# A hybrid attention block on one core: attention B normalised from split squares, and three stretches re-ordered

## The chip, the cores and the metric

The kernel runs on one core of one Trainium2 chip. The metric is device time in microseconds (us) of one execution; shorter is better. Before the change three runs took 741.76, 742.28 and 742.61 us, so the median is 742.28.

## What is computed

One layer for 512 tokens of width 1024, in float32: a combined projection of x, two attentions side by side, gates, an output projection, LayerNorm, a squared-ReLU MLP (1024 to 4096 to 1024) and a second LayerNorm. The part that the change rewrites is the end of attention B, which has four heads of value width 128:

```
def rms_norm(x, g):
    return x * lax.rsqrt(jnp.mean(jnp.square(x), axis=-1, keepdims=True) + RMS_EPS) * g

w   = softmax(q1 k1) - lam * softmax(q2 k2)          # per head, causal by chunks of 64
out = rms_norm(w @ v, subln_g) * (1 - lam_init)      # over the 128 columns of a head
```

Queries and keys of B are rotated first: of each 64 columns the first 16 are turned by an angle that depends on the position (`partial_rope`). Attention A has eight heads with a bias table and no rotation.

## The kernel before

Every float32 product is made of three matmuls. Each operand is split into a high part (a cast to fp32r on ACT, `split`, L82) and the rest (a subtraction on DVE, L83); then high times high, high times low and low times high are summed in PSUM. A matmul takes 128 rows by 512 columns. Weights come from memory as chunks of 128x1024 (`prefetch`, L107), each landing in one of three `raw` buffers and being split into one of three `wh` and three `wl` buffers; `chunk` (L144) hands out the next one and prefetches.

The order of the program: some matmuls on zeros while the first loads come in (`warm_up`); the projection, written as a generator (`proj`) that is advanced one step at a time; attention A in 36 steps with one projection step between two of them; attention B (`attn_b`) in 16 units (head, block of 128 queries) and a tail, with 1.8 projection steps between two units; then the two branch products, the output projection in two column groups, LayerNorm 1 inside the second group, the MLP and LayerNorm 2. Instructions are issued by a scheduler that keeps one order per engine: it may move an instruction ahead of others of its engine by its own priorities, unless `tc.keep_in_program_order` pins it. An engine then runs its list strictly in order, waiting where an operand or a buffer isn't ready.

A unit of B works as follows. PE makes two score blocks in `st` banks (L270, L271); DVE adds the mask and takes the maximum (L278), ACT takes exp (L280), DVE the reciprocal of the 128x1 sums (L282), POOL multiplies one map (L575), DVE subtracts (L576). Three units later (`LAG`) PE transposes the result (L289) into one of four `mm` banks, ACT copies it to `ph` (L296) and DVE writes the rest to `pl` (L297), which frees the bank. After the fourth unit of a head PE multiplies with the values (`pv`, L511 to L513) into `o`. `mean_sq` squares on ACT (L516), sums over the 128 rows of the head with eight plain matmuls of two columns against ones (L524), and computes 1/sqrt by an integer start and three Newton steps on 128x8 numbers (L527 to L538, thirteen DVE instructions). `normalise` spreads the 512 factors over all rows: POOL multiplies the identity with them (L547, two products), PE multiplies with ones (L552, two matmuls), and DVE forms the product with the head's output (L554), which is split.

The rotation (`rope`, L476) is four POOL instructions for a query or key tile, eight calls in all. The LayerNorm 1 part (`fin1`) adds on DVE (L735), takes statistics (L739), normalises (L805 on ACT, L806 on DVE), and PE transposes the rows (L817).

Of the kernel before, what the change touches and what calls it, by code (L numbers as in the profile page):

```python
# [40 lines left out]
def block_kernel(ctx, tc, w, x_t, x, pos, relb, bgate, lq1, lk1, lq2, lk2, subg,  # L41
# [38 lines left out]

    def split(src, h, l, eng=None):
        A.copy(out=h, in_=src)  # L82
        (eng or V).tensor_tensor(out=l, in0=src, in1=h.bitcast(F32), op=ALU.subtract)  # L83
# [4 lines left out]
    def load_x(k, cuts=((0, S),)):  # L88
        if k not in x_raw:
            x_raw[k] = e_tile()  # L90
        for lo, hi in cuts:
            nc.sync.dma_start(out=x_raw[k][:, lo:hi], in_=x_t[k * P:(k + 1) * P, lo:hi])
# [13 lines left out]

    def prefetch(n_dma, n_split):  # L107
        while dma_at[0] < min(NCH, n_dma):
            i = dma_at[0]
            raws[i] = wp.tile([P, 1024], F32, tag="raw", bufs=3, name=name("raw"))  # L110
            if i == 0:
                for j in range(2):
                    sl = slice(512 * j, 512 * (j + 1))
                    if j == 0:
                        load_x(0, ((0, P),))
                    nc.sync.dma_start(out=raws[i][:, sl], in_=w[i][:, sl])
                    load_x(j, ((P, S),) if j == 0 else ((0, S),))
            else:
                nc.sync.dma_start(out=raws[i], in_=w[i])
            dma_at[0] += 1  # L120
        while split_at[0] < min(NCH, n_split):
            i = split_at[0]
            if i in dest:
                hs, ls = dest[i]
                for j in range(2):
                    split(raws[i][:, 512 * j:512 * (j + 1)], hs[j], ls[j],
                          G if i in on_pool else V)
                parts[i] = (hs, ls)
            else:
# [26 lines left out]
    A.activation(ones_r, ones, AF.Copy, scale=128.0)  # L156
# [30 lines left out]
    def s_group(act_h, act_l, evac, before=None, nk=4, tail=1, cut_last=False):  # L187
# [13 lines left out]
        for c in range(nk):  # L201
            if before:
                before(c)
            wh, wl = chunk()
# [271 lines left out]
    def rope(t):  # L476
# [3 lines left out]
        G.tensor_tensor(out=a, in0=v[:, :, :, 0:16], in1=cos_t, op=ALU.mult)  # L480
# [16 lines left out]
    def attn_b():  # L497
# [3 lines left out]
        for which in range(2):  # L501
            rope(qb[which][0])
        ops[0] = prep_b(0)
        yield

        def pv(h):
# [8 lines left out]
            sq = e_tile()  # L515
            A.activation(sq, o, AF.Square)  # L516
            og = e_tile()
            A.activation(og, o, AF.Copy, scale=g8)
            return og, sq

        def mean_sq(og, sq):
            ms = mm_bank()
            for t in range(NT):
                T.matmul(ms[:, 2 * t:2 * t + 2], sq[:, t * P:(t + 1) * P], ones[:, 0:2],  # L524
                         start=True, stop=True)
            v, y, a = small(8), small(8), small(8)
            V.tensor_scalar(v, ms[:, 0:8], EPS, None, op0=ALU.add)  # L527
            V.tensor_scalar(y.bitcast(I32), v.bitcast(I32), -0.5, float(0x5f3759df),
                            op0=ALU.mult, op1=ALU.add)
            for _ in range(3):  # L530
                V.scalar_tensor_tensor(out=a, in0=y, scalar=-0.5, in1=y,
                                       op0=ALU.mult, op1=ALU.mult)
                V.tensor_tensor(out=a, in0=a, in1=v, op=ALU.mult)
                V.scalar_tensor_tensor(out=y, in0=a, scalar=1.5, in1=y,
                                       op0=ALU.add, op1=ALU.mult)
            rh, rl = small(8, FR), small(8, FR)
            V.tensor_copy(out=rh, in_=y)
            V.tensor_tensor(out=rl, in0=y, in1=rh.bitcast(F32), op=ALU.subtract)  # L538
            return og, sq, rh, rl

        def normalise(og, a, rh, rl):
            rb = mm_bank()
            for n, part in enumerate((rh, rl)):
                diag = vt()
                r = part.bitcast(F32)
                eye = ident[:, :]
                G.tensor_tensor(out=diag.rearrange("p (t q) -> p t q", q=P),  # L547
                                in0=bass.AP(tensor=eye.tensor, offset=eye.offset,
                                            ap=[eye.ap[0], [0, NT], [1, P]]),
                                in1=bass.AP(tensor=r.tensor, offset=r.offset,  # L550
                                            ap=[r.ap[0], [2, NT], [0, P]]), op=ALU.mult)
                T.matmul(rb, ones_r, diag, start=(n == 0), stop=(n == 1))  # L552

            V.tensor_tensor(out=a.rearrange("p (q n) -> p n q", n=NT),  # L554
                            in0=og.rearrange("p (n q) -> p n q", q=P),
                            in1=rb.rearrange("p (n q) -> p n q", q=P), op=ALU.mult)
            h_, l_ = vt(), vt()
            split(a, h_, l_)
            ob_h.append(h_)
            ob_l.append(l_)  # L560

        held = {}
        for i in range(len(units) + LAG + 7):
# [25 lines left out]
            for stage in (6, 3, 1):  # L589
                k = i - LAG - stage  # L590
                if 0 <= k < len(units) and k % NT == NT - 1:
# [3 lines left out]
                    elif stage == 3:  # L595
                        held[h] = mean_sq(*held[h])
# [65 lines left out]

    A.preload_act_table(AF.Exp)
    warm_up(6)
    prefetch(1, 0)
    rope_angles()
# [6 lines left out]
    advance(7)  # L673
# [7 lines left out]
    for i in range(36):  # L681
        next(steps_a, None)
        advance(1)
        if i == 32:
# [3 lines left out]
    for _ in range(16 + LAG + 7):  # L688
# [146 lines left out]
    for n, _ in enumerate(s_group(mh, ml, evac_res(0))):  # L835
        prefetch(c0 + 5, min(c0 + 3, next_chunk[0] + 3))
# [7 lines left out]
    for _ in s_group(mh, ml, fin1, tail=4):  # L844
# [141 lines left out]
```

## Time and profile before

| | |
|---|---|
| median of 3 runs | 742.28 us |
| profiled execution | 741.43 us |
| its span in the trace | 739.6 us |
| mean granted TensorE clock | 0.997 of full speed |

The span runs from the first to the last instruction of the trace; 1.8 us of the profiled execution lie around it. The trace gives each engine's instructions with start and length; PE is TensorE, DVE VectorE, ACT ScalarE, POOL GpSimd, SP the engine that issues most DMAs. Matmuls overlap, so what one costs is read from the distance between two starts, not from its length. An idle time in brackets is followed by what ended it.

### The profile page before, as it was taken

The numbers are of one execution on the slowest core, as the hardware profiler recorded it, in microseconds if no ns is written. First come the engines' busy times: TensorE is split into PE (matmuls) and PEld (weight loads), VectorE is DVE, ScalarE is ACT, GpSimd is POOL, SyncE is SP. The second block draws the span as 40 slices with busy tenths as digits, with TensorE's granted clock in tenths as the row PEclk, the third lists the DMA queues.
The fourth block names the chain that finished last, engine by engine and source line by source line (L and its number), as shares of the span: only waits on it lengthen the run. The fifth ranks groups of instructions, "written<-read, shape, count | busy, mean of one in ns | idle before, by whom it ended". The sixth has DMA issues, their size and how long they took to land.

```text
span 739.6 us, 9267 instructions
## 1 busy us (share of the span) xinstructions
PE 725.7 (98%) x3446; PEld 606.0 (82%) x3446; DVE 423.4 (57%) x831; ACT 283.6 (38%) x497; POOL 94.4 (13%) x127
## 2 busy tenths in 40 slices
PE   8999999999999999999999999999999999999995
PEld 6888888878888888888788888888888888888885
DVE  6566655546666764746876886423135655612545
ACT  5565654536565643224363223221212322312200
POOL 0023333550122121143000000000000000000001
PEclk9999999999999999999999999999999999999998
DMA  8553222212332222182502232322223223232302
GB/s 294 197 173 112 85 88 60 83 58 86 121 108 86 86 63 104 62 313 96 190 1 84 87 114 86 115 86 98 102 86 113 86 86 113 86 113 86 115 29 85
DMA packets 26940, 78.34 MB, mean 106 GB/s; under 512 B 4368, under 2 KB 5136, under 8 KB 26896
## 3 DMA queue, kind: packets, MB, share of 16 engines
q1 hardware_dynamic: 26176, 76.71, 31.3%
q10 hardware_dynamic: 720, 1.05, 0.4%
q8 instruction: 27, 0.44, 0.2%
q14 instruction: 17, 0.14, 0.1%
HBM read 71.45 MB, written 2.10 MB: 99 GB/s over the span
## 4 chain that ended last, share of the span: by engine, by line
PE 87%; DVE 4%; POOL 3%; ACT 2%; DMA 2%; issue 1%; SPq 0%; DVEq 0%; ACTq 0%; POOLq 0%
PE mm L178 11%; PE mm L180 11%; PE mm L179 11%; PE mm L183 7%; PE mm L185 7%; PE mm L184 7%; PE st L185 3%; PE st L184 3%; PE st L183 3%; PE st L180 3%; PE st L179 3%; PE st L178 3%; POOL G L629 2%; DMA raw<-in_w_dram 2%; PE st L271 1%; PE o L185 1%
## 5 line engine op out<-in xcount | busy, mean ns | idle before, releaser
L83 DVE TENSOR_TENSOR wl<-raw,wh 128x1024 fp32r<-128x1024 f32 (+1 forms) x115 | 140.2, 1219 | 128.5 <-ACT wh L82 128.4
L82 ACT CAST wh<-raw 128x1024 fp32r<-128x1024 f32 (+1 forms) x115 | 120.0, 1044 | 207.6 <-PE st L185 67.1
L183 PE MATMUL mm<-wh,X 128*128 128x512 f32 (+1 forms) x192 | 77.0, 401 | 1.9 <-ACT X L82 1.6
L178 PE MATMUL mm<-X,wh 128*128 128x512 f32 x192 | 76.9, 401 | 0.0
L179 PE MATMUL mm<-X,wh 128*128 128x512 f32 x192 | 74.9, 390 | 0.0
L180 PE MATMUL mm<-X,wl 128*128 128x512 f32 x192 | 74.9, 390 | 0.0
L184 PE MATMUL mm<-wl,X 128*128 128x512 f32 (+1 forms) x192 | 74.5, 388 | 0.0
L185 PE MATMUL mm<-wh,X 128*128 128x512 f32 (+1 forms) x192 | 74.2, 388 | 0.0
L783 POOL TENSOR_SCALAR s<-s 128x1 f32<-128x1 f32 x1 | 0.4, 409 | 388.8 <-DVE s L767 388.8
L178 PE MATMUL mm<-x1t_h,wh 128*128 128x512 f32 x128 | 49.8, 389 | 0.0
L179 PE MATMUL mm<-x1t_l,wh 128*128 128x512 f32 x128 | 49.8, 389 | 0.0
L180 PE MATMUL mm<-x1t_h,wl 128*128 128x512 f32 x128 | 49.8, 389 | 0.0
L280 ACT ACTIVATE e<-e,s 128x128 f32<-128x128 f32 (+3 forms) x64 | 36.1, 564 | 30.4 <-DVE s L278 30.0
L372 POOL TENSOR_SCALAR e<-e,s 128x128 f32<-128x128 f32 (+3 forms) x32 | 34.7, 1085 | 76.3 <-DVE s L282 76.3
L183 PEld LDWEIGHTS mm<-wh,X 128*128 128x128 f32 x192 | 36.2, 189 | 9.8 <-ACT X L82 2.7
L185 PEld LDWEIGHTS mm<-wh,X 128*128 128x128 f32 x192 | 36.0, 188 | 7.8 <-DVE X L83 0.3
L180 PEld LDWEIGHTS mm<-X,wl 128*128 128x128 f32 x192 | 36.0, 188 | 7.7
L178 PEld LDWEIGHTS mm<-X,wh 128*128 128x128 f32 x192 | 36.1, 188 | 6.9
L184 PEld LDWEIGHTS mm<-wl,X 128*128 128x128 f32 x192 | 36.2, 188 | 6.7 <-DVE wl L83 0.2
L179 PEld LDWEIGHTS mm<-X,wh 128*128 128x128 f32 x192 | 36.2, 188 | 6.5
L82 ACT CAST V<-lt 128x512 fp32r<-128x512 f32 x24 | 14.9, 621 | 62.8 <-DVE lt L858 62.8
L180 PE MATMUL st<-x1t_h,wl 128*128 128x512 f32 (+1 forms) x104 | 38.8, 373 | 0.0
(257 smaller groups left out, 1537.0 us busy)
## 6 DMA issues: line engine op xcount, KB each, us to landing
raw<-in_w_dram SPq DMA_DIRECT2D x119, 512.0 KB, 3.3
q<-q SPq DMA_DIRECT2D x32, 128.0 KB, 2.3
G<-in_relb_dram SPq DMA_DIRECT2D x8, 256.0 KB, 4.2
x<-in_x_dram SPq DMA_DIRECT2D x4, 512.0 KB, 7.6
e<-in_x_t_dram SPq DMA_DIRECT2D x7, 256.0 KB, 6.4
out_dram<-x SPq DMA_DIRECT2D x3, 256.0 KB, 2.0
out_dram<-x ACTq DMA_DIRECT2D x3, 256.0 KB, 2.1
raw<-in_w_dram SPq DMA_DIRECT2D x2, 256.0 KB, 3.2
```

The lines of the kernel that those rows point to most:

```text
L82: A.copy(out=h, in_=src)
L83: (eng or V).tensor_tensor(out=l, in0=src, in1=h.bitcast(F32), op=ALU.subtract)
L178: T.matmul(ps, lw_h, rh, start=first, stop=False)
L179: T.matmul(ps, lw_h, rl, start=False, stop=False)
L180: T.matmul(ps, lw_l, rh, start=False, stop=last)
L183: T.matmul(ps, ah, w_h, start=first, stop=False)
L184: T.matmul(ps, ah, w_l, start=False, stop=False)
L185: T.matmul(ps, al, w_h, start=False, stop=last)
L271: T.matmul(ps[:, :n], q2[:, sl], k1[:, :n], start=False, stop=True)
L280: A.activation(e[:, :n], e[:, :n], AF.Exp, bias=nm, scale=-1.0, accum_out=sums)
L372: G.tensor_scalar(ex[:, :n], ex[:, :n], r, None, op0=ALU.mult)
L629: G.tensor_tensor(out=m, in0=m, in1=g, op=ALU.add)
```

## The change

Four things change. (1) `pv` writes the squares twice on ACT, once as fp32 and once as fp32r, and DVE subtracts: a high and a low part. `normalise` sums them over the rows with two 128x512 matmuls against a matrix of 1/128, which at once spreads the mean over all rows; ACT takes the square root (with its table of functions loaded before, and the exp table again behind), DVE the reciprocal of all 128x512 numbers, and DVE multiplies. `mean_sq`, its matmuls, the Newton steps and the POOL products are gone, and normalising a head starts three units earlier. (2) Three weight splits of the first MLP chunks are pinned behind each step of LayerNorm 1. (3) The rotations are pinned: head 0's two at steps 22 and 30 of attention A, the others at the start of units 0 and 1 of the head before. (4) The first 128 columns of x^T are loaded by ACT's queue, chunk 1 of the weights is loaded and split in halves between the x^T pieces, rotary angles come later, and seven warm-up matmuls read a 128x128 tile.

```diff
@@ -78,18 +78,22 @@
     def o_bank():
         return bank("o")
 
+    pinned = [False]
+
     def split(src, h, l, eng=None):
         A.copy(out=h, in_=src)
-        (eng or V).tensor_tensor(out=l, in0=src, in1=h.bitcast(F32), op=ALU.subtract)
+        i = (eng or V).tensor_tensor(out=l, in0=src, in1=h.bitcast(F32), op=ALU.subtract)
+        if pinned[0]:
+            tc.keep_in_program_order(i)
+    def first_loads():
+
+        load_x(0, ((0, P),), A)
+        for i in range(2):
+            raws[i] = wp.tile([P, 1024], F32, tag="raw", bufs=3, name=name("raw"))
+            for j in range(2):
+                sl = slice(512 * j, 512 * (j + 1))
+                nc.sync.dma_start(out=raws[i][:, sl], in_=w[i][:, sl])
+                load_x(2 * i + j, ((P, S),) if i + j == 0 else ((0, S),))
+        dma_at[0] = 2
+
     def prefetch(n_dma, n_split):
         while dma_at[0] < min(NCH, n_dma):
             i = dma_at[0]
             raws[i] = wp.tile([P, 1024], F32, tag="raw", bufs=3, name=name("raw"))
-            if i == 0:
-                for j in range(2):
-                    sl = slice(512 * j, 512 * (j + 1))
-                    if j == 0:
-                        load_x(0, ((0, P),))
-                    nc.sync.dma_start(out=raws[i][:, sl], in_=w[i][:, sl])
-                    load_x(j, ((P, S),) if j == 0 else ((0, S),))
-            else:
-                nc.sync.dma_start(out=raws[i], in_=w[i])
+            nc.sync.dma_start(out=raws[i], in_=w[i])
...
-                if i == 0:
+                if i < 2:
                     for j in range(2):
                         sl = slice(512 * j, 512 * (j + 1))
                         split(raws[i][:, sl], h[:, sl], l[:, sl])
-                        split_x(j)
+                        split_x(2 * i + j)
                 else:
...
     def chunk(ahead=2):
         c = next_chunk[0]
-        prefetch(c + ahead + 1, c + ahead)
+        prefetch(c + ahead + 1, c + max(ahead, 1))
         next_chunk[0] += 1
         return parts.pop(c)
...
     def warm_up(n):
         ps = st_bank()
-        src = e_tile()
-        V.memset(src, 0.0)
+        src = e_tile()[:, 0:P].bitcast(FR)
+        V.memset(src.bitcast(F32), 0.0)
+        wide = bass.AP(tensor=src.tensor, offset=src.offset, ap=[src.ap[0], [0, NT], [1, P]])
         for _ in range(n):
-            T.matmul(ps, src[:, 0:P].bitcast(FR), src.bitcast(FR), start=True, stop=True)
+            T.matmul(ps.rearrange("p (a b) -> p a b", b=P), src, wide, start=True, stop=True)
...
-        G.tensor_tensor(out=a, in0=v[:, :, :, 0:16], in1=cos_t, op=ALU.mult)
+        tc.keep_in_program_order(
+            G.tensor_tensor(out=a, in0=v[:, :, :, 0:16], in1=cos_t, op=ALU.mult))
...
             rope(qb[which][0])
+            yield
         ops[0] = prep_b(0)
...
-            sq = e_tile()
+            sq, sq_h, sq_l = e_tile(), vt(), vt()
             A.activation(sq, o, AF.Square)
+            A.activation(sq_h, o, AF.Square)
             og = e_tile()
             A.activation(og, o, AF.Copy, scale=g8)
-            return og, sq
-
-        def mean_sq(og, sq):
-            ms = mm_bank()
-            for t in range(NT):
-                T.matmul(ms[:, 2 * t:2 * t + 2], sq[:, t * P:(t + 1) * P], ones[:, 0:2],
-                         start=True, stop=True)
-            v, y, a = small(8), small(8), small(8)
...
-            rh, rl = small(8, FR), small(8, FR)
-            V.tensor_copy(out=rh, in_=y)
-            V.tensor_tensor(out=rl, in0=y, in1=rh.bitcast(F32), op=ALU.subtract)
-            return og, sq, rh, rl
-
-        def normalise(og, a, rh, rl):
+            V.tensor_tensor(out=sq_l, in0=sq, in1=sq_h.bitcast(F32), op=ALU.subtract)
+            return og, sq, sq_h, sq_l
+
+        def normalise(og, a, sq_h, sq_l):
+
             rb = mm_bank()
...
-                                            ap=[eye.ap[0], [0, NT], [1, P]]),
-                                in1=bass.AP(tensor=r.tensor, offset=r.offset,
-                                            ap=[r.ap[0], [2, NT], [0, P]]), op=ALU.mult)
-                T.matmul(rb, ones_r, diag, start=(n == 0), stop=(n == 1))
-
-            V.tensor_tensor(out=a.rearrange("p (q n) -> p n q", n=NT),
+            for n, part in enumerate((sq_h, sq_l)):
+                T.matmul(rb, ones_r, part, start=(n == 0), stop=(n == 1))
+            A.activation(a, rb, AF.Sqrt, bias=epst)
+            V.reciprocal(a, a)
+
+            b = e_tile()
+            V.tensor_tensor(out=b.rearrange("p (q n) -> p n q", n=NT),
                             in0=og.rearrange("p (n q) -> p n q", q=P),
-                            in1=rb.rearrange("p (n q) -> p n q", q=P), op=ALU.mult)
+                            in1=a.rearrange("p (n q) -> p n q", q=P), op=ALU.mult)
             h_, l_ = vt(), vt()
-            split(a, h_, l_)
...
-        for i in range(len(units) + LAG + 7):
+        for i in range(len(units) + LAG + 4):
             if i < len(units):
                 h, t = units[i]
                 n = (t + 1) * P
+                if t < 2 and h < 3:
+                    rope(qb[t][h + 1])
...
-                if t == 1 and h < 3:
-                    for which in range(2):
-                        rope(qb[which][h + 1])
...
-            for stage in (6, 3, 1):
+            for stage in (3, 1):
                 k = i - LAG - stage
                 if 0 <= k < len(units) and k % NT == NT - 1:
                     h = units[k][0]
                     if stage == 1:
                         held[h] = pv(h)
-                    elif stage == 3:
-                        held[h] = mean_sq(*held[h])
                     else:
...
         def before(c):
-            if c:
+            for k in (2 * c + 2, 2 * c + 3):
+                if 0 < c and k < KD:
+                    load_x(k)
+            if c > 1:
                 for k in (2 * c, 2 * c + 1):
-                    load_x(k)
                     split_x(k)
         yield from s_group(xh, xl, evac_va, before)
...
-    A.preload_act_table(AF.Exp)
-    warm_up(6)
-    prefetch(1, 0)
-    rope_angles()
+    warm_up(7)
+    first_loads()
+    tc.keep_in_program_order(A.preload_act_table(AF.Exp))
     main = proj()
 
     def advance(n):
         for _ in range(n):
             next(main, None)
 
-    advance(7)
+    advance(2)
+    tc.keep_in_program_order(A.activation(ones_r, ones, AF.Copy, scale=1.0))
+    rope_angles()
+    advance(5)
     rope_tables()
     lam_and_gains()
     advance(1)
@@ -681,11 +669,11 @@
     for i in range(36):
         next(steps_a, None)
         advance(1)
-        if i == 32:
...
     for n, _ in enumerate(s_group(mh, ml, evac_res(0))):
-        prefetch(c0 + 5, min(c0 + 3, next_chunk[0] + 3))
+        prefetch(c0 + 5, min(c0 + 4, next_chunk[0] + 3))
     fin = evac_res(1)
 
     def fin1(s, ps, lo, hi):
@@ -841,7 +829,10 @@
         ln1(s)
         if s:
             x1_transposed(s - 1)
-    for _ in s_group(mh, ml, fin1, tail=4):
+        pinned[0] = True
+        prefetch(c0 + 7, c0 + 4 + min(s + 1, 3))
+        pinned[0] = False
+    for _ in s_group(mh, ml, fin1, tail=4, ahead=0):
```

The start, on SP, the loads behind the first x^T and weight pieces (`raw` weights, `e` x^T pieces); first before, then after:

```order
L119 DMA raw_168<-in_w_dram 128x1024
L119 DMA raw_170<-in_w_dram 128x1024
L92 DMA e_216<-in_x_t_dram 128x512
L92 DMA e_222<-in_x_t_dram 128x512
L119 DMA raw_228<-in_w_dram 128x1024
L92 DMA e_258<-in_x_t_dram 128x512
L92 DMA e_264<-in_x_t_dram 128x512
```
```order
L96 DMA e_116<-in_x_t_dram 128x512
L118 DMA raw_118<-in_w_dram 128x512
L96 DMA e_120<-in_x_t_dram 128x512
L118 DMA raw_118<-in_w_dram 128x512
L96 DMA e_123<-in_x_t_dram 128x512
L126 DMA raw_130<-in_w_dram 128x1024
L403 DMA s_187<-in_pos_dram 128x4
L96 DMA e_232<-in_x_t_dram 128x512
L96 DMA e_234<-in_x_t_dram 128x512
```

The third x^T piece stood behind both whole weight chunks (1024 columns each); it now stands behind half a chunk (512 columns).

The end of attention A, on POOL (L480 to L485 are one rotation, `e` tiles at L372, after at L379, are attention's multiplies); before, then after:

```order
L480 TENSOR_TENSOR s_2209<-G_1490,cos_t 128x128
L481 TENSOR_TENSOR s_2210<-G_1490,sin_t 128x8x8
L483 TENSOR_TENSOR s_2210<-G_1490,sin_t 128x8x8
L485 TENSOR_TENSOR G_1490<-s_2209,s_2210 128x8x16
L480 TENSOR_TENSOR s_2487<-G_1184,cos_t 128x128
L481 TENSOR_TENSOR s_2488<-G_1184,sin_t 128x8x8
L372 TENSOR_SCALAR e_1561<-e_1561,s_1566 128x128
L483 TENSOR_TENSOR s_2488<-G_1184,sin_t 128x8x8
L485 TENSOR_TENSOR G_1184<-s_2487,s_2488 128x8x16
```
```order
L379 TENSOR_SCALAR e_1519<-e_1519,s_1524 128x512
L379 TENSOR_SCALAR e_1571<-e_1571,s_1576 128x128
L379 TENSOR_SCALAR e_1609<-e_1609,s_1614 128x256
L379 TENSOR_SCALAR e_1638<-e_1638,s_1643 128x384
L488 TENSOR_TENSOR s_1671<-G_1498,cos_t 128x128
L489 TENSOR_TENSOR s_1672<-G_1498,sin_t 128x8x8
L491 TENSOR_TENSOR s_1672<-G_1498,sin_t 128x8x8
L493 TENSOR_TENSOR G_1498<-s_1671,s_1672 128x8x16
L379 TENSOR_SCALAR e_1680<-e_1680,s_1685 128x512
L488 TENSOR_TENSOR s_1855<-G_1186,cos_t 128x128
```

Three rotations and more stood directly ahead of the multiply of e_1561; now the same multiply (e_1571) has attention's multiplies ahead of it, and the rotation of G_1498 comes three multiplies later.

The normalising of head 0, on DVE (s 128x8 are the Newton steps; e_2368 the squares, then the root, then its reciprocal); before, then after:

```order
L297 TENSOR_TENSOR pl_2346<-mm_2499,ph_2345 128x3x128
L527 TENSOR_SCALAR s_2510<-mm_2505 128x8
L282 RECIPROCAL s_2481<-s_2478 128x1
L528 TENSOR_SCALAR s_2511<-s_2510 128x8
L574 TENSOR_SCALAR s_2483<-s_2481,lam 128x1
L531 SCALAR_TENSOR_TENSOR s_2512<-s_2511 128x8
L533 TENSOR_TENSOR s_2512<-s_2512,s_2510 128x8
L534 SCALAR_TENSOR_TENSOR s_2511<-s_2512,s_2511 128x8
L576 SCALAR_TENSOR_TENSOR e_2466<-e_2466,s_2471,e_2476 128x256
L531 SCALAR_TENSOR_TENSOR s_2512<-s_2511 128x8
L533 TENSOR_TENSOR s_2512<-s_2512,s_2510 128x8
L534 SCALAR_TENSOR_TENSOR s_2511<-s_2512,s_2511 128x8
```
```order
L304 TENSOR_TENSOR pl_2350<-mm_2507,ph_2349 128x3x128
L538 RECIPROCAL e_2368<-e_2368 128x512
L289 RECIPROCAL s_2501<-s_2498 128x1
L541 TENSOR_TENSOR e_2518<-e_2373,e_2368 128x4x128
L563 TENSOR_SCALAR s_2503<-s_2501,lam 128x1
L285 ISA e_2566,s_2567<-st_2563,maskb 128x384
L285 ISA s_2567 128x1
L565 SCALAR_TENSOR_TENSOR e_2486<-e_2486,s_2491,e_2496 128x256
L85 TENSOR_TENSOR V_2521<-e_2518,V_2520 128x512
L262 SCALAR_TENSOR_TENSOR q_2592<-mm_2587,q_2592 64x512
L289 RECIPROCAL s_2571<-s_2568 128x1
L285 ISA e_2576,s_2577<-st_2573,maskb 128x384
```

And on ACT in the same place, before, then after:

```order
L280 ACTIVATE e_2466,s_2468<-e_2466,s_2467 128x256
L296 CAST ph_2345<-mm_2499 128x3x128
L280 ACTIVATE e_2476,s_2478<-e_2476,s_2477 128x256
L607 ACTIVATE G_2565<-mm_2540,bg 128x512
L280 ACTIVATE e_2570,s_2572<-e_2570,s_2571 128x384
L254 ACTIVATE q_2596<-mm_2591 64x512
L296 CAST ph_2345<-mm_2619 128x4x128
L280 ACTIVATE e_2580,s_2582<-e_2580,s_2581 128x384
```
```order
L287 ACTIVATE e_2486,s_2488<-e_2486,s_2487 128x256
L303 CAST ph_2349<-mm_2507 128x3x128
L537 ACT_TABLE_LOAD
L537 ACTIVATE e_2368<-mm_2513,epst 128x512
L287 ACT_TABLE_LOAD
L287 ACTIVATE e_2496,s_2498<-e_2496,s_2497 128x256
L591 ACTIVATE G_2561<-mm_2536,bg 128x512
L261 ACTIVATE q_2592<-mm_2587 64x512
L84 CAST V_2520<-e_2518 128x512
L303 CAST ph_2349<-mm_2615 128x4x128
```

The short Newton rows are replaced by one 128x512 reciprocal and the product, ahead of the mask rows (L285) and of the last `pl`; on ACT two table loads and the root stand ahead of the unit's second exp.

## Rows read from the trace of the kernel before

**Rows 1.** The page: PE's busy line, and GB/s in forty slices.
```profile
PE 725.7 (98%) x3446; PEld 606.0 (82%) x3446; DVE 423.4 (57%) x831; ACT 283.6 (38%) x497; POOL 94.4 (13%) x127
...
GB/s 294 197 173 112 85 88 60 83 58 86 121 108 86 86 63 104 62 313 96 190 1 84 87 114 86 115 86 98 102 86 113 86 86 113 86 113 86 115 29 85
```
**Rows 2.** Timeline of ACT (start, length, instruction, idle and releaser), 10.0 to 12.2.
```profile
10.48 1.04 ACT L82 CAST wh<-raw 128x1024 fp32r<-128x1024 f32 x1 [0.60 <-DMA raw<-in_w_dram]
11.44 1.14 ACT L82 CAST X<-e 128x512 fp32r<-128x512 f32 x2
```
**Rows 3.** Timeline of PE, 9.8 to 12.6.
```profile
10.09 0.40 PE L185 MATMUL mm<-wh,X 128*128 128x512 f32 x1
12.10 0.50 PE L183 MATMUL mm<-wh,X 128*128 128x512 f32 x1 [1.61 <-ACT X L82]
```
**Rows 4.** Timeline of POOL, 140 to 152.5: first rotation row, attention A's multiply behind the rotations.
```profile
140.67 0.46 POOL L480 TENSOR_TENSOR s<-G,cos_t 128x128 f32<-128x128 f32 x1 [0.81 <-ACT G L467]
...
151.32 0.60 POOL L372 TENSOR_SCALAR e<-e,s 128x128 f32<-128x128 f32 x1
```
**Rows 5.** Timeline of PE, 148.5 to 153.5.
```profile
150.33 0.39 PE L271 MATMUL st<-q,q 128*128 128x512 f32 x1
151.98 0.33 PE L289 MATMUL st<-ident,e 128*128 128x128 f32 x1 [1.25 <-POOL e L372]
...
152.76 0.50 PE L352 MATMUL o<-pl,V 128*128 128x512 f32 x1 [0.22 <-DVE pl L297]
```
**Rows 6.** Timeline of PE, 226.5 to 228.
```profile
226.85 0.95 PE L524 MATMUL mm<-ones,e 128*128 128x2 f32 x8
227.67 0.48 PE L178 MATMUL mm<-X,wh 128*128 128x512 f32 x1
```
**Rows 7.** Groups of DVE by line and form: count, busy us, mean ns, idle before.
```profile
L533 DVE TENSOR_TENSOR s<-s,s 128x8 f32<-128x8 f32 x12 | 2.0, 167 | 0.4
...
L554 DVE TENSOR_TENSOR e<-e,mm 128x512 f32<-128x512 f32 x4 | 4.2, 1062 | 0.0
...
L83 DVE TENSOR_TENSOR V<-e,V 128x512 fp32r<-128x512 f32 x8 | 5.5, 686 | 1.4 <-ACT V L82 1.4
...
L282 DVE RECIPROCAL s<-s 128x1 f32<-128x1 f32 x64 | 10.3, 161 | 21.0 <-ACT e L280 16.1 <-POOL e L372 4.6
...
L447 DVE TENSOR_SCALAR lam<-lam 128x1 f32<-128x1 f32 x1 | 0.2, 153 | 0.0
L449 DVE TENSOR_SCALAR g<-g 128x1 f32<-128x1 f32 x1 | 0.1, 146 | 0.0
```
**Rows 8.** Timeline of ACT, at heads 0, 1 and 2, and at the last table load.
```profile
228.05 0.47 ACT L296 CAST ph<-mm 128x384 fp32r<-128x384 f32 x1
...
233.41 0.69 ACT L607 ACTIVATE G<-mm,bg 128x512 f32<-128x512 f32 x1 [3.98 <-PE mm L180]
...
254.43 0.46 ACT L296 CAST ph<-mm 128x384 fp32r<-128x384 f32 x1
...
279.33 0.47 ACT L296 CAST ph<-mm 128x384 fp32r<-128x384 f32 x1
...
313.43 1.28 ACT L697 ACT_TABLE_LOAD   x1
```
**Rows 9.** DVE's busy time in one stretch: window, length, busy us and instructions.
```profile
229.12:237.22 8.10, 5.48 (x25) 1.00 0.20 67
```
**Rows 10.** Timeline of PE, at heads 0, 1 and 2.
```profile
238.89 0.27 PE L289 MATMUL mm<-ident,e 128*128 128x128 f32 x1
...
267.99 0.40 PE L512 MATMUL o<-pl,V 128*128 128x512 f32 x1
...
291.38 0.39 PE L512 MATMUL o<-pl,V 128*128 128x512 f32 x1
```
**Rows 11.** Timeline of DVE, 362.5 to 364.
```profile
362.69 1.21 DVE L83 TENSOR_TENSOR wl<-raw,wh 128x1024 fp32r<-128x1024 f32 x1
```
**Rows 12.** Waits of PE: line, releaser, us in total, times, longest.
```profile
PE mm L817 <- ACT lt L805: 1.0, 1, 1.0
```

More of the change, by code (lines that the diff above doesn't have):

```diff
@@ L79, in o_bank, with load_x @@
         return bank("o")
+    pinned = [False]
     def split(src, h, l, eng=None):
         A.copy(out=h, in_=src)
-        (eng or V).tensor_tensor(out=l, in0=src, in1=h.bitcast(F32), op=ALU.subtract)
+        i = (eng or V).tensor_tensor(out=l, in0=src, in1=h.bitcast(F32), op=ALU.subtract)
+        if pinned[0]:
+            tc.keep_in_program_order(i)
     xh, xl, x_raw = [], [], {}
-    def load_x(k, cuts=((0, S),)):
+    def load_x(k, cuts=((0, S),), q=nc.sync):
         if k not in x_raw:
@@ L91, in load_x @@
         for lo, hi in cuts:
-            nc.sync.dma_start(out=x_raw[k][:, lo:hi], in_=x_t[k * P:(k + 1) * P, lo:hi])
+            q.dma_start(out=x_raw[k][:, lo:hi], in_=x_t[k * P:(k + 1) * P, lo:hi])
     def split_x(k):
@@ L155, in block_kernel @@
     ones_r = const.tile([P, P], FR, name="ones_r")
-    A.activation(ones_r, ones, AF.Copy, scale=128.0)
     epst = const.tile([P, 1], F32, name="epst")
@@ L185, in smm, with s_group @@
         T.matmul(ps, al, w_h, start=False, stop=last)
-    def s_group(act_h, act_l, evac, before=None, nk=4, tail=1, cut_last=False):
+    def s_group(act_h, act_l, evac, before=None, nk=4, tail=1, cut_last=False, ahead=2):
         jobs = [(s, 0, S) for s in range(NT)]
@@ L203, in s_group @@
                 before(c)
-            wh, wl = chunk()
+            wh, wl = chunk(ahead)
             if c >= nk - tail:
@@ L514, in pv @@
                          stop=(j == NT - 1))
-            sq = e_tile()
+            sq, sq_h, sq_l = e_tile(), vt(), vt()
             A.activation(sq, o, AF.Square)
+            A.activation(sq_h, o, AF.Square)
             og = e_tile()
             A.activation(og, o, AF.Copy, scale=g8)
-            return og, sq
-        def mean_sq(og, sq):
-            ms = mm_bank()
-            for t in range(NT):
-                T.matmul(ms[:, 2 * t:2 * t + 2], sq[:, t * P:(t + 1) * P], ones[:, 0:2],
-                         start=True, stop=True)
-            v, y, a = small(8), small(8), small(8)
[L527 to L535, printed above, removed]
-            rh, rl = small(8, FR), small(8, FR)
-            V.tensor_copy(out=rh, in_=y)
-            V.tensor_tensor(out=rl, in0=y, in1=rh.bitcast(F32), op=ALU.subtract)
-            return og, sq, rh, rl
@@ L541, in normalise @@
-        def normalise(og, a, rh, rl):
-            rb = mm_bank()
[L543 to L548, printed above, removed]
-                                            ap=[eye.ap[0], [0, NT], [1, P]]),
-                                in1=bass.AP(tensor=r.tensor, offset=r.offset,
-                                            ap=[r.ap[0], [2, NT], [0, P]]), op=ALU.mult)
-                T.matmul(rb, ones_r, diag, start=(n == 0), stop=(n == 1))
-            V.tensor_tensor(out=a.rearrange("p (q n) -> p n q", n=NT),
+            V.tensor_tensor(out=sq_l, in0=sq, in1=sq_h.bitcast(F32), op=ALU.subtract)
@@ L557, in normalise @@
             h_, l_ = vt(), vt()
-            split(a, h_, l_)
+            split(b, h_, l_)
             ob_h.append(h_)
@@ L683, in block_kernel @@
         advance(1)
-        if i == 32:
+        if i in (22, 30, 32):
             next(steps_b)
@@ L687, in block_kernel @@
     due = 0.0
-    for _ in range(16 + LAG + 7):
+    for _ in range(16 + LAG + 4):
         next(steps_b, None)
```

## The prediction

> **What bounds the kernel now.** I read the page's busy line first, then PE's waits, then a timeline around each place that the change touches. PE is busy 98% of the span [rows 1]: it is the bound, and the other engines count only where PE waits for them. So the sum has two kinds of terms: matmul time that goes away, and waits of PE that go away or come. It is made against the profiled execution (741.43 us, 0.85 below the median of the runs, 742.28), whose span of 739.6 is nearly all PE; I apply the difference to the median.
>
> **The start.** PE starts a matmul at 10.09 and the next at 12.10, idle 1.61 of it until ACT's cast of an x^T piece [rows 3]. That cast begins at 11.44, directly behind a 1.04 us cast of a whole weight chunk that itself waited for its transfer [rows 2]. After the change the third x^T piece has half a chunk ahead of it that it shares the queue with, where it had two whole ones: 0.75 MB less to come first. At the 294 GB/s of the first slice [rows 1] that is 2.6 us earlier, and its cast has only half-chunk casts ahead of it. That is more than the whole wait, so the wait goes: 1.8, between the idle 1.61 and the full distance of 2.01. The first x^T piece on ACT's queue costs an issue ahead of a table load that nothing waits for; the seventh warm-up matmul takes the place of the time saved by clearing a narrower tile. I take nothing for both. What is late next is the second x^T piece of that chunk, needed twelve matmuls later.
>
> **The rotations.** From 140.67 POOL works off rotations one behind the other, and attention A's multiply gets its turn only at 151.32 [rows 4]. PE waits for it: 150.33 to 151.98 with 1.25 idle, and 0.22 more at 152.76 for the `pl` that follows from the same multiply [rows 5]. Pinned a few multiplies apart, a rotation holds up one multiply by its own four instructions instead of a row of them. Take 1.6, between the idle times (1.47) and the distance of 1.65 plus 0.22. The six later calls now stand in attention B ahead of a unit's multiply (L575), whose result PE wants three units later; I take nothing for them, and 1.6 back if that cover fails.
>
> **The sum of squares.** Eight two-column matmuls take PE 0.82 us, 226.85 to 227.67 [rows 6]; four heads make 3.3. The two wide matmuls of `normalise` stay as they were, only earlier, in the place of the eight. The squares' second pass on ACT and the subtraction on DVE (0.69 [rows 7]) fall into the units between `pv` and `normalise`, where neither engine is waited for; at nothing.
>
> **LayerNorm 1.** PE waits 1.0 for the normalised rows (L817 behind L805) [rows 12]. DVE was behind: the split of an MLP chunk ran at 362.69 for 1.21, ahead of the last residual sum of the first block [rows 11]. Pinned behind that block's normalising, the sum starts 1.2 earlier, more than the wait. I take 1.0. The split that moves is needed later, in the MLP.
>
> These four give 1.8 + 1.6 + 3.3 + 1.0 = 7.7 us.
>
> **What the new normalising costs.** DVE loses thirteen Newton instructions a head (0.167 each [rows 7], 2.2 together) and gains a product (1.06 as L554 was [rows 7]) in another place, and one instruction that the trace doesn't show: a reciprocal of 128x512, R. From below it is bounded by any other 128x512 pass, 0.69 (L83 [rows 7]). From above: one element costs 161 ns as a reciprocal and 146 or 153 as a multiply (L282, L449, L447 [rows 7]). If the 8 ns over L447 are the price of each element, R = 0.15 + 512 x 0.008 = 4.25; with the 15 over L449 it is 7.8. The ends are far apart; the nearest row is the same opcode's, L282, best compared with L447, the slower of the two multiplies: I take 4.25. The Trainium skill (VectorE: DVE Perf Modes, First, the fixed hardware budget) says that Reciprocal is an iterative divide with a repeat count of 8; at that page's 0.96 GHz this would be an estimated 4.3 us, and the sum by it is the forecast's; no run here shows it yet, and the rows alone would also allow one pass.
>
> Now the walk for head 0. ACT ends a cast at 228.52 (228.05 + 0.47) and is then all but idle until 233.41 [rows 8]. In that hole stand a table load (1.28, L697 [rows 8]) and the root, which I price as the activation of the same shape (0.69, L607 [rows 8]): done at 230.5. DVE spent 5.48 us on work between 229.12 and 237.22 [rows 9], where `pl` of the head's last transposes was done; 3.3 of it stays, the product and a split (1.06 + 0.69) come forward, so `pl` is done at 230.5 + R + 5.05 = 239.8. PE wants that bank at 238.89 [rows 10], less 0.4 since eight short matmuls gave way to two wide ones in the head's place: 238.5. PE waits 1.3. Head 1: the cast ends at 254.89 [rows 8], the root at 256.9, `pl` by the same sum at 266.2; PE wants it at 267.99 [rows 10] less 0.4: no wait, 1.4 to spare. Head 2: cast done 279.80 [rows 8], root 281.8; behind R stand two whole weight splits (1.21 each, as L83 in [rows 11]), the product, a gate product, the split and `pl` (1.06 and three of 0.69): 291.6, against 291.38 [rows 10] less 0.4, or 291.0: waits 0.6. Head 3 has no units behind it, and the branch product wants its result only some 45 matmuls later; nothing. Together 1.9. The second table load, ahead of the unit's second exp, delays a map that PE transposes three units later; at nothing.
>
> Sum: 7.7 - 1.9 = 5.8 faster: 735.6 by the profiled execution, **736.5** by the median.
>
> **The rivals.**
> *The reciprocal is one pass* (0.69). Every `pl` above comes 3.6 us earlier and no head waits: 742.28 - 7.7 = 734.6, and 733.9 if the start and the rotations give their whole distances. For it: one element costs nearly as little as a multiply. Against it: at one element the reciprocal is still dearer than either multiply, by 8 and 15 ns [rows 7].
>
> *Table loads cost twice their row.* If ACT stands for another 1.28 behind each load, the roots come 1.28 later: head 0 waits 2.6, head 2 1.9, head 1 still nothing, 4.5 in all: 739.1. The one load that stands directly behind a cast in the trace takes 1.28 with no idle time ahead of it [rows 8]; what follows it isn't shown there. The Trainium skill (ScalarE: Activation LUTs, What ACT_TABLE_LOAD costs) gives 1283 ns and a drain of some 1380 for every switch, and tells one to batch by table set, which this change does not. By that rule the time is this rival's; the trace agrees on the load and shows no drain.
>
> *A wait gives way to the next.* At the start and in attention A four or five transfers and queues run close together; if POOL's rotations now hold the multiply of an attention B unit, or the second x^T piece is late, 1.6 to 3.4 come back: 738.1 to 739.9. For it: before the rotation stood first in the queue for 10 us and PE waited only at its end [rows 4, 5], so there is slack of some us; this speaks against it too.
>
> *Slower: the reciprocal holds DVE at every head.* At 7.8 head 0 waits 4.9, head 1 2.2, head 2 4.2: 11.3 against 7.7, or 745.9. It decides from R = 6.6, where the three waits together reach 7.7. For it only the lower of two multiply rows [rows 7].
>
> *It does not do what it says:* if PE's sum of squares was hidden in time that PE would have waited anyway, the 3.3 shrink. But PE stands at no wait in those stretches of the timeline [rows 6], so this has little weight.
>
> **How the numbers follow.** Forecast 0.48 (its own range 735.1 to 737.9: waits of 0.5 to 3.3); one pass 0.20; table loads 0.10; a wait given back 0.14; slower 0.06; 0.02 for the last. The range of 733.6 to 740.0 leaves out the slower case and the ends of the others. No change to be told from noise is within 0.2%, 1.5 us: faster means below 740.8. That takes in the forecast, one pass and nearly all of the next two: 0.88; same 0.06, slower 0.06.
>
> **What would show it.** Right: no PE wait over 0.5 us near 10 to 12 and at the rotations, none for L805's rows; no PE matmul of two columns; a DVE reciprocal of about 4.2 us at each head, and waits of PE behind `pl` at heads 0 and 2. Wrong: a reciprocal under 1 us or over 6, an idle ACT behind a table load, PE waiting for a unit's multiply in attention B, or the wait at 12 only moved to the next x^T piece.

## The result, and the profile after

The changed kernel takes 736.24 us (median of six runs, 734.53 to 736.95) against 742.25 for the kernel before: a ratio of 0.9913, 95% interval 0.9899 to 0.9927. The forecast was 736.5. The profiled execution is the fastest of the six, 734.53 us with a span of 732.7, so its gain of 6.9 is larger than that of the medians, 6.0; why the runs spread by 2.4 us is a question that the experiments take up.

The page's busy line after (total us, share of the span and instructions of each engine), and all waits of PE (line, releaser, us in total, times, longest):

```profile
PE 721.3 (98%) x3415; PEld 603.0 (82%) x3415; DVE 432.0 (59%) x788; ACT 295.7 (40%) x512; POOL 89.3 (12%) x119
```
```profile
PE mm L296 <- DVE pl L304: 1.4, 1, 1.4
PE st L252 <- DVE e L249: 1.0, 1, 1.0
PE mm L189 <- ACT wh L84: 0.8, 1, 0.8
PE mm L189 <- DVE q L262: 0.3, 1, 0.3
```

PE has 4.4 us less to do than in [rows 1]. The waits of [rows 3, 5, 12] are gone; two are new, 1.4 behind the last `pl` of head 0 and 0.8 ahead of the first real matmul. PE's timeline after at the places of [rows 5], [rows 6] and LayerNorm 1 (start, length, instruction):

```profile
149.15 0.27 PE L296 MATMUL st<-ident,e 128*128 128x128 f32 x1
...
149.49 0.40 PE L359 MATMUL o<-pl,V 128*128 128x512 f32 x1
...
223.28 0.49 PE L296 MATMUL mm<-ident,e 128*128 128x128 f32 x3
223.52 0.72 PE L536 MATMUL mm<-V,ones_r 128*128 128x512 f32 x2
224.08 0.40 PE L184 MATMUL mm<-X,wh 128*128 128x512 f32 x1
...
360.51 1.04 PE L805 MATMUL mm<-ident,lt 128*128 128x128 f32 x8
```

No idle time stands in brackets in any of them. Lined up instruction by instruction with the trace of before, PE gains 1.9 at the rotations, 3.4 over four heads from the sums of squares and 1.0 at LayerNorm 1; it loses 1.5 at head 0. With 1.4 at the start that is 6.2 of the 6.9; the rest is in pieces of under 0.5 that I did not follow.

### The profile page after: what moved, and what is told of

The parts are those of the page before. It is cut to its first block, busy times and chain, and to the rows that moved or that the text cites. A ratio compares the mean times of both kernels' runs of the same rounds, so it can differ in the third digit from the quotient of the medians.

```text
span 732.7 us, 9157 instructions
## 1 busy us (share of the span) xinstructions
PE 721.3 (98%) x3415; PEld 603.0 (82%) x3415; DVE 432.0 (59%) x788; ACT 295.7 (40%) x512; POOL 89.3 (12%) x119
## 4 chain that ended last, share of the span: by engine, by line
PE 95%; DVE 2%; ACT 1%; issue 1%; DMA 0%; POOL 0%; DVEq 0%; POOLq 0%; ACTq 0%
PE mm L184 11%; PE mm L186 11%; PE mm L185 11%; PE mm L189 9%; PE mm L190 9%; PE mm L191 9%; PE st L190 4%; PE st L191 4%; PE st L189 4%; PE st L185 3%; PE st L184 3%; PE st L186 3%; PE o L190 2%; PE o L191 1%; PE o L189 1%; PE st L278 1%
## 5 line engine op out<-in xcount | busy, mean ns | idle before, releaser
L379 POOL TENSOR_SCALAR e<-e,s 128x128 f32<-128x128 f32 (+3 forms) x32 | 34.7, 1086 | 84.5 <-DVE s L289 84.5
```

The lines of the kernel that those rows point to most:

```text
L379: G.tensor_scalar(ex[:, :n], ex[:, :n], r, None, op0=ALU.mult)
```

## The experiments

**Each part undone.** Four kernels, each the changed one with one part as before; in short:

```
old_norm:  pv / mean_sq / normalise of before, stages (6, 3, 1)
old_ln1:   - prefetch(c0 + 7, ...) pinned in fin1; ahead=0
old_rope:  - keep_in_program_order, - yield; rope after t == 1 again
old_start: prefetch(1, 0), whole second chunk, six warm-up matmuls, x^T on SP
```

> The changed kernel with the normalising of before (eight two-column matmuls, Newton steps, POOL products), all else as changed. Theory (the terms add up, and the norm is worth 3.4 us of matmuls less a 1.4 us wait at head 0): about 738.2 us, 2.0 above the changed kernel's 736.24; no PE wait behind pl near 236. Rival (the norm's matmuls lie in time that PE would wait anyway, so the norm is worth nothing or costs): 736.3 or less.

Measured: 738.93 (ratio to before 0.9951, 0.9936 to 0.9965), 2.7 above the changed kernel; no wait behind `pl`. The rival fell: the norm is worth at least its matmuls less the wait, 3.4 - 1.4 = 2.0; what the other 0.7 is I did not follow.

> The changed kernel with LayerNorm 1's splits left to the scheduler as before. Theory: PE waits about 1.0 us again for L805's row, and the time is about 737.3. Rival (the wait had come from something upstream that the other parts have also moved): no wait comes back, 736.2.

Measured: 737.31 (0.9926, 0.9912 to 0.9939), 1.1 above; the wait is back, 0.7 of idle time where 1.0 was expected. The time is as the theory said.

> The changed kernel with the rotations unpinned and where they were. Theory: POOL's queue of rotations holds attention A's multiply again and PE waits 1.25 + 0.2 us near 150, 1.9 by distances: about 738.1. Rival (in attention B the pinned rotations cost what they save in attention A, through POOL's multiply there): 736.3, with PE's waits in attention B smaller.

Measured: 737.68 (0.9935, 0.9922 to 0.9949), 1.4 above. Its waits of PE:

```profile
PE st L296 <- POOL e L379: 1.3, 1, 1.3
...
PE mm L296 <- DVE pl L304: 0.7, 1, 0.7
```

The wait on POOL is back in full, 1.3 and 0.2 behind it, and head 0's wait is half of the changed kernel's: what the theory names is twice as large as what the rival names. But the rival's reason isn't seen. In the changed kernel POOL's multiplies at head 0 start after idle time, waiting for DVE, and not behind a rotation. What differs is ACT: with the rotations pinned, its cast of `ph` starts 1.98 us behind PE's sum of squares (225.50 and 223.52), in `old_rope` 1.29 and before 1.20 (228.05 [rows 8] and 226.85 [rows 6]). Which earlier row makes it late I did not follow. In `old_rope`, PE, then ACT:

```profile
226.89 0.72 PE L534 MATMUL mm<-V,ones_r 128*128 128x512 f32 x2
...
228.18 0.46 ACT L303 CAST ph<-mm 128x384 fp32r<-128x384 f32 x1
```

> The changed kernel with loads, splits and warm-up of before. Theory: the first matmul comes 0.7 us earlier (4.3 instead of 5.0) and the wait of 1.6 idle near 10 comes back, 1.3 in sum: about 737.5. Rival (the late first piece costs more than the trace shows, since the first matmuls run on halves): 736.5 or less.

Measured: 736.54 (0.9921, 0.9906 to 0.9935; runs 735.75 to 737.57), 0.3 above, which these runs can't tell from nothing. The rival's 736.5 fits. The profile has the wait of 1.4 back and the first matmul at 4.32. So the theory failed by size. (The intervals of the last three kernels overlap that of the changed one, so for the single parts the traces weigh more than the times.) The next rows are PE's timelines of the last warm-up and the first real matmuls in the changed kernel and then in `old_norm`, whose start is the same:

```profile
2.91 1.30 PE L252 MATMUL st<-e 128*128 128x512 f32 x3
...
4.98 0.92 PE L189 MATMUL mm<-wh,X 128*128 128x512 f32 x2 [0.77 <-ACT wh L84]
5.74 0.47 PE L190 MATMUL mm<-wl,X 128*128 128x512 f32 x1
6.05 0.40 PE L191 MATMUL mm<-wh,X 128*128 128x512 f32 x1
6.28 0.39 PE L190 MATMUL mm<-wl,X 128*128 128x512 f32 x1
```
```profile
2.92 1.48 PE L252 MATMUL st<-e 128*128 128x512 f32 x3
...
5.11 1.22 PE L189 MATMUL mm<-wh,X 128*128 128x512 f32 x2 [0.72 <-ACT wh L84]
6.13 0.63 PE L190 MATMUL mm<-wl,X 128*128 128x512 f32 x1
6.56 0.63 PE L191 MATMUL mm<-wh,X 128*128 128x512 f32 x1
...
8.70 0.56 PE L191 MATMUL mm<-wh,X 128*128 128x512 f32 x1
9.09 0.40 PE L189 MATMUL mm<-wh,X 128*128 128x512 f32 x1
9.32 0.39 PE L190 MATMUL mm<-wl,X 128*128 128x512 f32 x1
```

In the second, matmuls of 512 columns stand 0.43 us apart until 8.70 and 0.23 after: the lower of the clock's two levels, 1.2 GHz, then the upper, 2.4. The column of the granted clock shows 1.00 in both stretches, and over the warm-up, whose matmuls also start 0.43 apart; so at the start only the distances tell.

In all profiles with this start PE's warm-up ended at 4.2 to 4.4 and PE then idled 0.55 to 0.9 us. Eight such profiles were taken: in four the slow pace lasted 7 to 11 matmuls, and the 49th real matmul started at 17.7 to 18.4; in the others it started at 16.3 to 17.3. The length of the idle stretch doesn't tell them apart: it is 0.55 to 0.72 in the slow four and 0.66 to 0.88 in the others. What nearly does is the last warm-up matmul. In three of the others it is already short, 0.44 to 0.51 us (the three warm-ups above end at 2.91 + 1.30 = 4.21), and in the four slow profiles and the fourth of the others, `stage2`, it takes 0.63. The profile models the ends of matmuls, so this is a sign and no proof. By it, PE had reached the upper level in those three before it idled, and in the slow four the idle time fell ahead of the rise. That the idle time holds the rise back is argued, not shown.

Before the change the 49th real matmul started at 17.66, the 25th at 12.10 [rows 3]. Against that the part gains 0.4 to 1.4 in one half of the profiles and loses 0.1 to 0.7 in the other. The start of before varies too: in `old_start`, the only other profile of it, the 49th started at 19.06.

**The start, mended in two ways.**

```diff
-    warm_up(7)                       # warm9
+    warm_up(9)
-        load_x(0, ((0, P),), A)      # x0a_sp: the piece is loaded on SP, behind the first weight piece
```

> The changed kernel with nine warm-up matmuls instead of seven, so that PE works on until about 5.05 and doesn't idle between the warm-up and the first real matmul (4.2 to 5.0 or 5.1). Theory (that idle stretch is why matmuls of most runs start 0.43 us apart until 8.6 to 10.2 instead of 0.23): the first real matmuls stand 0.23 apart from the second or third on, no wait near 10, time about 734.5, 1.7 under the changed kernel. Rival (the slow pace is chance, with or without the idle time): 736.2, spread as before.

Measured: 735.42 (734.94 to 735.72; 0.9908, 0.9894 to 0.9922), 0.8 better than the changed kernel where 1.7 was expected; the intervals overlap, so by the times alone the gain isn't shown. PE's timeline:

```profile
3.34 1.91 PE L252 MATMUL st<-e 128*128 128x512 f32 x4
5.12 0.79 PE L189 MATMUL mm<-wh,X 128*128 128x512 f32 x1
...
6.43 0.57 PE L191 MATMUL mm<-wh,X 128*128 128x512 f32 x1
6.84 0.40 PE L189 MATMUL mm<-wh,X 128*128 128x512 f32 x1
7.07 0.40 PE L190 MATMUL mm<-wl,X 128*128 128x512 f32 x1
```

With no idle stretch the pace is 0.23 from the fourth matmul on. The spread of the runs is 0.8 where it was 2.4, but these are four runs against six.

> The changed kernel with the first 128 columns of x^T again on SP's queue, behind the first weight piece, as before; chunk 1 in halves stays. Theory (ACT's queue lands that piece later, 4.1 against 3.55): the first matmul at 4.3, no idle stretch ahead of it, full pace, no wait near 10; about 734.2. Rival (the transfers behind it come later by as much, or the pace stays slow all the same): a wait near 10 of 0.4 or more, 735.8 to 736.2.

Measured: 735.17 (734.63 to 735.46; 0.9904, 0.9891 to 0.9918), 1.1 better, between the theory's 734.2 and the rival's 735.8; here too the intervals overlap. The first matmul starts at 4.42 and the pace is full, but a wait comes:

```profile
8.58 0.50 PE L188 MATMUL mm<-wh,X 128*128 128x512 f32 x1 [0.77 <-ACT X L84]
```

So the theory holds for the clock and the first piece, and the rival for the transfers behind it: what PE gains ahead of them it waits for. Of five profiles without the idle stretch (these two, the two below with nine warm-ups, and `old_start`, which has before's) none has the slow pace beyond the third matmul, against four of eight with it. This speaks for the theory; with so few profiles it doesn't prove it.

**Head 0's wait.** ACT and then DVE in the changed kernel, at head 0:

```profile
224.99 0.51 ACT L287 ACTIVATE e<-e,s 128x256 f32<-128x256 f32 x1 [0.58 <-DVE s L285]
...
225.50 0.46 ACT L303 CAST ph<-mm 128x384 fp32r<-128x384 f32 x1
225.98 1.28 ACT L537 ACT_TABLE_LOAD   x1
227.27 0.69 ACT L537 ACTIVATE e<-mm,epst 128x512 f32<-128x512 f32 x1
227.98 1.28 ACT L287 ACT_TABLE_LOAD   x1
229.27 0.51 ACT L287 ACTIVATE e<-e,s 128x256 f32<-128x256 f32 x1
```
```profile
227.99 3.35 DVE L538 RECIPROCAL e<-e 128x512 f32<-128x512 f32 x1 [1.08 <-ACT e L537]
...
231.38 1.08 DVE L541 TENSOR_TENSOR e<-e,e 128x512 f32<-128x512 f32 x1
...
233.64 0.48 DVE L565 SCALAR_TENSOR_TENSOR e<-e,s,e 128x256 f32<-128x256 f32 x1 [0.68 <-POOL e L564]
234.05 0.69 DVE L85 TENSOR_TENSOR V<-e,V 128x512 fp32r<-128x512 f32 x1
...
236.02 0.69 DVE L304 TENSOR_TENSOR pl<-mm,ph 128x512 fp32r<-128x512 f32 x1
```

From 227.99 DVE works almost without a gap until `pl` ends at 236.71; PE takes the bank at 236.76 after 1.37 idle. The 0.68 is a loop: the unit's last multiply on POOL waits for a row of DVE that stands behind the reciprocal (L563), and DVE then waits for POOL. Two kernels take one part of this away, one moves it, one doubles it.

```diff
-            V.reciprocal(a, a)                          # no_recip
+            V.tensor_scalar(a, a, 1.0, None, op0=ALU.mult)
-            A.activation(a, rb, AF.Sqrt, bias=epst)     # no_table
+            A.activation(a, rb, AF.Identity, bias=epst)
-            for stage in (3, 1):                        # stage2
+            for stage in (2, 1):
+            V.reciprocal(a, a)                          # two_recip: a second one
```

> The changed kernel with the reciprocal left out: a 128x512 multiply by one in its place on DVE, the tables and the root as they are. Theory (DVE's 3.35 us are the cause of head 0's wait): no wait of PE behind pl. Rival (the second table load ahead of the unit's exp, and POOL's and DVE's rows behind it, are the cause): a wait of 0.5 to 1.4 us stays.

Measured: one run, 733.54; no wait behind `pl`. As the theory said.

> The changed kernel with the root left out (the mean plus epsilon is passed on), so that the three pairs of table loads go, 2.57 us a head on ACT; the reciprocal stays. Theory (head 0's reciprocal starts 1.3 earlier, and the unit's second exp 2.6 earlier): the wait of 1.4 behind pl falls to 0 to 0.2, time 734.9 from a median of 736.24. Rival (only DVE's time counts, ACT is off the path): the wait stays at 1.0 or more.

Measured: one run, 734.53; the wait falls to 0.3, just over what the theory allowed. PE's sum of squares, ACT's second exp and two rows of DVE:

```profile
224.50 0.72 PE L536 MATMUL mm<-V,ones_r 128*128 128x512 f32 x2
...
227.56 0.51 ACT L287 ACTIVATE e<-e,s 128x256 f32<-128x256 f32 x1
...
227.86 3.33 DVE L538 RECIPROCAL e<-e 128x512 f32<-128x512 f32 x1
...
233.53 0.48 DVE L565 SCALAR_TENSOR_TENSOR e<-e,s,e 128x256 f32<-128x256 f32 x1 [0.69 <-POOL e L564]
```

Counted from PE's sum of squares, the reciprocal starts 3.36 behind it, where it was 4.47 (223.52 to 227.99): 1.1 earlier, and that is what the wait lost. So the first load is in the chain beside DVE's 3.35, and to take either away is enough or nearly so. The second load isn't: without it the exp comes 2.7 earlier, and DVE still waits 0.69 for POOL, since POOL waits for the DVE row behind the reciprocal and the product.

> The changed kernel with a head normalised one unit earlier (stage 2 instead of 3). Theory (head 0's 1.4 us wait comes from the reciprocal standing in the unit ahead of the next head's query and key preparation, where DVE's queue is full): the wait behind pl goes or falls under 0.4, time about 735.0. Rival (any place in the units has the 3.35 us reciprocal ahead of a pl): a wait of 1 us or more at another place, 736.2 or more.

Measured: 743.89 (1.0023, 1.0011 to 1.0035), slower than the kernel before. The theory's wait behind `pl` went, but not its time; the rival's wait at another place came, but not for its reason: PE waited for the squares. Its waits of PE, PE's timeline at head 0, and PE's row for 220.10 to 223.20 (length, busy time and matmuls, granted clock, DMA share, GB/s):

```profile
PE mm L536 <- DVE V L529: 4.1, 2, 2.1
PE mm L536 <- ACT V L526: 1.2, 1, 1.2
```
```profile
220.09 0.79 PE L536 MATMUL mm<-V,ones_r 128*128 128x512 f32 x1 [1.96 <-DVE V L529]
220.68 0.63 PE L184 MATMUL mm<-X,wh 128*128 128x512 f32 x1
221.11 0.63 PE L185 MATMUL mm<-X,wh 128*128 128x512 f32 x1
...
223.60 0.39 PE L185 MATMUL mm<-X,wh 128*128 128x512 f32 x1
```
```profile
220.10:223.20 3.10, 3.10 (x7) 0.50 0.00 0
```

One unit earlier the squares aren't split. And the wait costs twice: behind 1.96 us of idle time, matmuls stand 0.43 apart for 3.1 us, and here the granted clock says so: 0.50 of full speed, the lower level. Behind the wait of 2.10 at 276.23 it is 0.50 for another 5.0 us. The two prices add up, by an estimate from these rows: 5.3 of waits, less the 1.4 that went, and half of 8.1 us are 7.9, where the times differ by 7.7. The changed kernel's wait of 1.37 shows no such stretch behind it (1.00 from 236.70 to 240.00).

> The changed kernel with a second 128x512 reciprocal of the first's result, so DVE has 3.35 us more at each head (the output is thereby another). Theory (cover at heads 0, 1, 2 as walked in the prediction: at 6.7 head 0 has 3.35 more than now, head 1 has 1 and head 2 has 3): PE waits 4.7, 1 and 3 us, the time is 742 to 745, and matmuls behind waits of 2 us and more stand 0.43 apart for a stretch. Rival (the wait at head 0 isn't the reciprocal's and the heads have more cover): waits under 4 in all, 736 to 740.

Measured: one run, 744.43; PE waits 4.3 in two pieces (1.77 and 2.5) for the masks (L285) at heads 0 and 1, three more waits of 0.3 to 0.5, nothing for head 2. The time came out in the range of the theory, the waits did not, neither in sum (5.6, not 8.7) nor in place: head 1 has less cover than I walked, head 2 more. Behind the 2.53 the granted clock was 0.50 from 273.10 to 276.40, behind the 1.77 it stayed at 1.00.

**Moving the work behind `pl`.** Nine warm-ups, and the reciprocal, product and split emitted one unit after the root. In `late_warm9` the scheduler leaves the reciprocal where it was, ahead of the last `pl` (228.72), so only the product and the split move; in `late_pin_warm9` it is pinned and moves too:

```diff
-            for stage in (3, 1):
+            for stage in (4, 3, 1):      # 3: sums and root; 4: divide(), but at once for head 3
+        def divide(og, a):
+            V.reciprocal(a, a)           # late_pin_warm9: in tc.keep_in_program_order(...)
```

> Nine warm-up matmuls, and the product with the head's output, its cast and split emitted one unit later than the root (stage 4, but for the last head); by the order of instructions the reciprocal stays where it was and the product and the split move behind the last pl. Theory (head 0's wait is DVE's row of reciprocal, product and split ahead of pl; 1.08 + 0.69 gone from the row are more than the wait of 1.4): no wait behind pl, about 734.0, 1.4 under nine warm-ups alone (735.42). Rival (POOL's multiply and DVE's row behind it hold pl, not the sum of DVE's work): the wait stays above 0.7, 735.0 or more.

Measured: **734.89** (734.51 to 735.80; 0.9910, 0.9897 to 0.9924): the lowest median here, 1.35 under the changed kernel, 0.5 under nine warm-ups alone (that much is within the spread). The theory's 734.0 and the rival's 735.0 lie on either side; the wait decides for the theory, since the 1.4 is gone. Two of 0.4 and 0.3 have come, the first at 41.85, far from this place, the second at 275.88:

```profile
PE st L277 <- DVE q L262: 0.4, 1, 0.4
PE mm L184 <- DVE pl L304: 0.3, 1, 0.3
```

> The same with the reciprocal pinned, so that it too stands behind the last pl of the head, ahead of three of the next head's four query and key rows. Theory (whatever stands behind the 3.35 us reciprocal waits; here the query and key rows and the next masks): no wait behind pl at head 0, but one of PE behind q or st rows of 0.3 to 2; 734.0 to 736.0. Rival (with pl out of the way nothing else is close): no wait, 734.0, as with the product alone moved.

Measured: 737.17 (0.9947, 0.9935 to 0.9960), 1.8 above nine warm-ups alone and over the theory's range. `pl` holds nothing, but the rows behind the reciprocal do, and further back than named: a weight split.

```profile
PE mm L186 <- DVE wl L85: 1.7, 1, 1.7
PE st L277 <- DVE q L262: 0.6, 1, 0.6
```

## Why the prediction was right, point by point

The time and the direction were right, and so was the shape: four gains on PE's path and one new wait at head 0. The sizes were not all right, and that the sum came so close is in part luck.

- *The sum of squares*, 3.3: 3.4 by the traces. *LayerNorm 1*, 1.0: 1.0 by the traces, 1.1 by undoing it. *The rotations*, 1.6: 1.9 by the traces, 1.4 by undoing them, since head 0's wait is then smaller. No wait of PE in attention B is for a unit's multiply; what the pinning costs at head 0 stands below.
- *The start*, 1.8: the mis-sized term. It measured 0.3. "I take nothing for both" failed: the first x^T piece on ACT's queue landed at 4.09 and was cast at 4.11, ahead of the weight cast, which so came at 4.32 (3.41 before); the weight piece had itself landed later, at 3.91 (3.39 before). So the first matmul moved from 4.28 to about 5.0. PE idled, and half of the profiles then show it at half pace. The wait near 10 did go.
- *The reciprocal*: 3.35, not 4.25.

```profile
L538 DVE RECIPROCAL e<-e 128x512 f32<-128x512 f32 x4 | 13.4, 3352 | 3.8 <-ACT e L537 3.8
```

  Per element that is (3352 - 153) / 512 = 6.2 ns; the 8 ns from [rows 7] came closer than the 15, but not for the reason given: L447 is an addition, so L449 is the only multiply of the two, and by it R was 7.8. The Trainium skill's repeat count of 8 (VectorE: DVE Perf Modes, First, the fixed hardware budget) would have made it an estimated 4.3 at that page's 0.96 GHz: the measurement decides, nearer to that estimate than to one pass.
- *Head 0's wait*, 1.3: measured 1.4, but by two errors that cancel. At 3.35 the walk gives 0.4. What it left out: ACT's cast ahead of the first load came some 0.8 later than in [rows 8], counted from PE's sum of squares (1.98 against 1.20), since DVE, behind with weight splits, let the first exp wait (0.58); without the pinned rotations it is in time and the wait 0.7. And from the reciprocal's end to `pl`'s it took 5.4 instead of 5.05, with 0.68 of DVE waiting for POOL in it. The second table load was rightly taken "at nothing": `no_table` has that wait without it.
- *Heads 1 and 2*: none and 0.6; none was seen. The covers behind that were wrong, as the doubled reciprocal showed.
- *The table loads*: the rival falls. The root starts at 227.27, where the load of 225.98 ends, and the reverse load is followed at 229.27 just so: 1.28 each, with no drain beside it. The first load of a head still costs, by its own length; that rival's price for it, one row, was in the forecast.

The medians agree because the start gave 1.5 less than I had taken and the norm more: the prediction nets 3.3 - 1.9 = 1.4 for it, and undoing it costs 2.7. Such errors need not cancel. One sum of the prediction is off as well: the one-pass rival with the whole distances is 742.28 - 8.2 = 734.1, not 733.9.

## What to carry to other kernels

When a new instruction is put on an engine whose queue is strictly in order, its price is not its length but what stands behind it: list the rows behind it up to the one PE wants, with the round trips through other engines among them. Moving a wait's cause to a place with "room" needs the same list at the new place: one unit earlier cost 7.7 us and pinned one unit later 1.8, while moving only the product and its split cost nothing. A gap of PE can cost more than the gap: behind waits of 2 us in the midst of work the clock stood at its lower level for 3 to 5 us more, and at the start a gap may fall ahead of the rise. So keep TensorE at work until its data is there, and judge a start by several profiles, since one may be the lucky kind.

## What the runs showed of the hardware that I had not expected

- An idle stretch of 0.55 to 0.9 us between warm-up and work was followed by 7 to 11 matmuls 0.43 us apart in four profiles of eight, and not in the others; in three of those others the last warm-up matmul was already at the quicker pace. The granted clock's column showed 1.00 throughout the start, also where matmuls stood 0.43 apart.
- Behind waits of 1.96, 2.10 and 2.53 us in the midst of work the granted clock was 0.50 for 3.1, 5.0 and 3.3 us (`stage2`, `two_recip`); behind waits of 1.37, 1.71 and 1.77 us it stayed at 1.00 (the changed kernel, `late_pin_warm9`, `two_recip`).
- A 128x512 float32 reciprocal on DVE takes 3.35 us, nearly five times a subtraction of that shape (0.69) and three times the product (1.08).
- The first 128 columns of x^T, issued on ACT's queue at 0.72, landed at 4.09; issued on SP's queue behind the first weight piece at 1.16 (`x0a_sp`) they landed at 3.71. The weight piece, issued on SP at 0.73 in both, landed at 3.91 and 3.53.
